# Hybrid diffusion layer on one core: the first stage loads its modulation weights into later h tiles, takes the sample's x first, halves its first block and moves the prompt's norm into its loop

## The chip, the cores and the metric

The kernel runs on one core of one Trainium2 chip. The metric is the device time of one execution in microseconds (us). Matrix products run on TensorE (PE in the profile), elementwise work on VectorE (DVE), ScalarE (ACT) and GpSimd (POOL); transfers are issued from the queue of SyncE (SP) and, for some, from that of ScalarE.

## What is computed

One layer for two groups of tokens that share their weights: 256 prompt tokens and 1024 sample tokens of width 1024. The part of the reference that the change touches is the first norm with its modulation and the first columns of the input projection:

```
def rmsnorm(x, g):
    return x * lax.rsqrt(jnp.mean(x * x, axis=-1, keepdims=True) + EPS) * g

mod_ctx = silu(c_ctx) @ w_ada + b_ada          # prompt's modulation, 6 x 1024
mod_lat = silu(c) @ w_ada + b_ada              # sample's modulation
h = rmsnorm(x, g_norm1) * (1.0 + scale_m) + shift_m
proj = h @ w_in                                # then convolutions, a state space scan,
                                               # an output projection and a gated ConvFFN
```

All arithmetic is float32. A product is made of three: each operand is split into hi (rounded to fp32r) and lo (the rest), and hi·hi, hi·lo and lo·hi are added in PSUM.

## The kernel before

The channels of x lie on partitions: x is eight blocks (k = 0 to 7) of 128 channels, each a tile of 128x1024 for the sample (`xs[k]`) and a quarter of a 128x4x256 tile for the prompt (`xp[k // 4][:, k % 4]`). Everything from line 89 to line 348 is the first stage. It must turn x into h (`hs_hi`, `hs_lo` for the sample, `hp_hi`, `hp_lo` for the prompt), and while it does so it already makes the sample's product with the two first column tiles of w_in (`N_LOOP = 2`, accumulators `pps`).

The front of the stage (lines 92 to 274): four small loads (`sm`, `cst`, `rows`), then the prompt's x (line 246) and the sample's (line 259), all on SP's queue. The prompt's squares and their sums over channels come first (lines 249 to 255). Then each sample tile is squared on ScalarE as it lands (line 261) and added on VectorE; a product with a matrix of ones (line 266) sums over partitions. Lines 271 and 272 make the reciprocal roots `rp` and `rs` with Ln and Exp on ScalarE.

`ada_block(k)` (lines 285 to 304) makes block k's shift and scale: it loads 1 MB of modulation weights into one of two halves of the tile `xq` (line 288, so the load for k waits until block k-2's products have read that half), makes eight small products (line 292), copies the sum (line 295), transposes it (line 298), and reduces and adds it on VectorE (lines 299 to 304, by the helpers at lines 77 and 83) to `mod` and `aff`.

The loop (lines 317 to 348) does for each k: load and split of the two weight tiles (lines 318 to 322), `ada_block(k + 1)`, the sample's x times scale and `rs` on VectorE (line 326, helper at line 80), hi on ScalarE (line 328), lo on VectorE (line 329), twelve products of 512 columns (line 337), and for the prompt a scaling by `rp` at k = 0 and 4 (line 341), hi on ScalarE (342), the value on VectorE (343), and at k = 3 and 7 the lo half on GpSimd (348) and the products for dt (`dtmm`, line 311). Behind the loop come the prompt's dt products and then the projection's column tiles in turn, whose weights are loaded and split by `wload` (lines 155 to 158).

The instructions are put in order for each engine when the kernel is built, by program order and by what is ready in the builder's own estimate; on the chip each engine keeps that order. A tile tag with n buffers hands a buffer on when the last reader of its former tile is done. `after(a, b)` adds an order between two instructions without a semaphore.

Of the kernel before, what the change touches and what calls it, by code (L numbers as in the profile page):

```python
# [6 lines left out]
F32 = mybir.dt.float32  # L7
F32R = mybir.dt.float32r
# [47 lines left out]
def body(nc, tc, A):  # L56
# [35 lines left out]
    dma(sm[:, wff1:], A["sm"][:, wff1:])  # L92
    dma(sm[:, 0:wff0], A["sm"][:, 0:wff0])
# [6 lines left out]
    dma(cst, A["cst"][:, : 128 + 40])  # L100
# [3 lines left out]
    dma(rows, A["rows"])  # L104
# [5 lines left out]
    act(arow, rows[:, 0:1], AF.Exp)  # L110
    ts(arow, arow, -1.0, None, ALU.mult, ALU.bypass)
    sc = T(con, [P, KT, 32], "sc", 1)
    V.memset(sc, 0.0)
    act(sc[:, :, 0:2], smv("cc").rearrange("p (k v) -> p k v", v=2), AF.Silu)
# [127 lines left out]
    xT = A["xT"]  # L242

    xp = [T(cv, [P, 4, TP], "xl", 2) for _ in range(2)]
    for q in range(2):
        dma(xp[q], xT[:, 4 * q:4 * q + 4, 0:TP])
    accp = T(sd, [P, 4, TP], "bc", 4)
    sqp = T(sd, [P, 4, TP], "bc", 4)
    act(accp, xp[0], AF.Square)
    act(sqp, xp[1], AF.Square)  # L250
    tt(accp, accp, sqp, ALU.add)
    tt(accp[:, 0:2], accp[:, 0:2], accp[:, 2:4], ALU.add)
    pr_p = pst()
    for i in range(2):
        nc.tensor.matmul(pr_p[:, 0:TP], ones, accp[:, i], start=i == 0, stop=i == 1)
    xs = [T(sd, [P, TS], "bcs", 4) if k < 4 else T(nrm, [P, TS], "x", 4) for k in range(KT)]
    acc_s = T(sd, [P, TS], "bc", 4)
    for k in range(KT):
        dma(xs[k], xT[:, k, TP:TT])
        q = T(cv, [P, TS], "cv", 4) if k else acc_s  # L260
        sq = act(q, xs[k], AF.Square)
        if k:
            tt(acc_s, acc_s, q, ALU.add)
    pr_s = [psa(), psa()]
    for i in range(2):
        nc.tensor.matmul(pr_s[i], ones, acc_s[:, i * 512:(i + 1) * 512], start=True, stop=True)
    tab = lnexp_table(sq)
    rp = T(cv, [P, TP], "cv", 4)
    rs = T(cv, [P, TS], "cv", 4)
    for r, a, b, src in ((rp, 0, TP, pr_p[:, 0:TP]), (rs, 0, 512, pr_s[0]), (rs, 512, TS, pr_s[1])):  # L270
        after(act(r[:, a:b], src, AF.Ln, scale=1.0 / D, bias=epsc), tab)
        act(r[:, a:b], r[:, a:b], AF.Exp, scale=-0.5)
    wdt = T(sd, [P, 640], "toks", 1)[:, 0:KT * 32].rearrange("p (k r) -> p k r", r=32)
    dma(wdt, A["w_dt"])


    hp_hi = [T(sd, [P, 4, TP], "bc", 4, F32R) for _ in range(2)]
    hp_lo = [T(sd, [P, 4, TP], "bc", 4, F32R) for _ in range(2)]
    hs_hi, hs_lo = [], []
    modv = mod.rearrange("p (b k) v -> p b k v", k=KT)  # L280
    badav = smv("bada").rearrange("p (b k) -> p b k", k=KT)

    xq = T(xy, [P, 4, TS], "xs", 1)

    def ada_block(k):
        wa = [xq[:, 2 * (k % 2) + i].rearrange("p (j c) -> p j c", j=4) for i in range(2)]
        for i in range(2):
            dma(wa[i], A["w_ad1"][k, i])
        pm = psa()
        for j in range(KT):  # L290
            q = 32 * (j % 4)
            nc.tensor.matmul(pm[q:q + 32, 0:2 * P], sc[:, j, :], wa[j // 4][:, j % 4, :],
                             start=j < 4, stop=j >= 4, skip_group_check=True, tile_position=(0, q))
        s = T(cv, [P, 2 * P], "cv", 4)
        act(s, pm[:, 0:2 * P], AF.Copy)
# [9 lines left out]

    def dtmm(pd, ks, h, n):
# [8 lines left out]
    pps = []  # L315
    ada_block(0)
    for k in range(KT):
# [1020 lines left out]
```

## Time and profile before

| what | us |
|---|---|
| median of 3 runs | 1551.56 |
| lowest and highest of the runs | 1550.9, 1554.01 |
| the profiled execution's own time | 1551.87 |
| its span, first to last instruction | 1550.1 |
| mean granted TensorE clock | 0.996 |

The profile is of one execution. Its span is the time from the first to the last instruction; 1.8 us of its time lie outside. A row of a timeline gives the start, the length, the engine, the line, the output and the inputs, how many were merged into the row, and in brackets how long the engine had been idle and what released it.

### The profile page before, as it was taken

Reading aid. Unit: us, or ns where it says so; the run is one execution under the profiler, and the core shown is the slowest. Engines: PE = TensorE matmul, PEld = TensorE weight load, DVE = VectorE, ACT = ScalarE, POOL = GpSimd, SP = SyncE. Lnnn points to the kernel's source line nnn. Section 1 sums busy time; section 2 is a strip of 40 time slices with the busy share of each in tenths; the row PEclk is TensorE's granted clock in tenths of the full one; section 3 lists DMA queues with packets and bytes.
Section 4 is the critical chain, followed back from the end, with each engine's and each line's share of the span. In section 5 each row is a group of like instructions: output and inputs, shape, how many; then the busy total and the mean of one; then the engine's idle time right before and its main releaser. Section 6 shows DMA issues by size and latency. Waiting matters only on the chain. (4 is left out here: it accounts for less than half of the span.)

```text
span 1550.1 us, 22496 instructions
## 1 busy us (share of the span) xinstructions
PE 1506.0 (97%) x8706; PEld 1287.7 (83%) x8706; DVE 1095.9 (71%) x1634; ACT 631.0 (41%) x1002; POOL 515.5 (33%) x289
## 2 busy tenths in 40 slices
PE   4999999999999999999999999999999999999997
PEld 2578887878888888888888888888888888888886
DVE  5765344288887467996666697556679978798696
ACT  6545334165654244433233342333334333433333
POOL 0432321111110003333333333333346554545452
PEclk9999999999999999999999999999999999999999
DMA  8635752444336413221222242122433323342221
GB/s 303 238 109 185 249 204 91 136 143 143 130 123 247 155 66 125 77 69 67 74 68 74 74 159 83 55 67 67 148 121 107 105 90 108 107 155 89 95 79 62
DMA packets 90652, 187.79 MB, mean 121 GB/s; under 512 B 9746, under 2 KB 37298, under 8 KB 90546
## 3 DMA queue, kind: packets, MB, share of 16 engines
q1 hardware_dynamic: 84722, 183.22, 34.8%
q10 hardware_dynamic: 5824, 3.15, 0.7%
q8 instruction: 68, 1.11, 0.3%
q14 instruction: 38, 0.31, 0.1%
HBM read 163.70 MB, written 22.63 MB: 120 GB/s over the span
## 5 line engine op out<-in xcount | busy, mean ns | idle before, releaser
L80 DVE SCALAR_TENSOR_TENSOR cc<-acc,sm,cc 128x504 f32<-128x504 f32 (+5 forms) x836 | 546.1, 665 | 110.8 <-ACT cc L1078 52.6
L77 POOL TENSOR_TENSOR wlo<-raw,whi 128x1024 fp32r<-128x1024 f32 (+2 forms) x91 | 211.5, 2324 | 637.1 <-ACT whi L157 444.2
L157 ACT ACTIVATE whi<-raw 128x1024 fp32r<-128x1024 f32 x97 | 102.6, 1058 | 247.3 <-PE acc L168 191.9
L80 DVE SCALAR_TENSOR_TENSOR x<-dn,mod,x 128x288 f32<-128x288 f32 (+2 forms) x176 | 96.2, 547 | 95.0 <-PE dn L170 94.4
L77 POOL TENSOR_TENSOR dlo<-draw,dhi 128x512 fp32r<-128x512 f32 (+1 forms) x88 | 108.8, 1237 | 89.8 <-ACT dhi L1131 89.7
L77 POOL TENSOR_TENSOR wlx<-raw,whx 128x1024 fp32r<-128x1024 f32 (+2 forms) x36 | 84.6, 2351 | 140.9 <-ACT whx L157 132.2
L166 PE MATMUL acc<-ya,whi 128*128 128x512 f32 (+1 forms) x400 | 119.0, 355 | 0.8 <-ACT cv L894 0.8
L168 PE MATMUL acc<-ya,whi 128*128 128x512 f32 (+1 forms) x400 | 118.9, 355 | 0.0
L170 PE MATMUL acc<-ya,wlo 128*128 128x512 f32 (+1 forms) x400 | 118.9, 354 | 0.0
L170 PE MATMUL acc<-oa,wlo 128*128 128x512 f32 (+1 forms) x400 | 118.8, 354 | 0.0
L168 PE MATMUL acc<-oa,whi 128*128 128x512 f32 (+1 forms) x400 | 118.7, 354 | 0.0
L166 PE MATMUL acc<-oa,whi 128*128 128x512 f32 (+1 forms) x400 | 118.3, 353 | 0.0
L166 PE MATMUL dn<-yb,dhi 128*128 128x288 f32 (+2 forms) x352 | 110.1, 313 | 5.3 <-DVE x L80 4.1
L168 PE MATMUL dn<-yb,dhi 128*128 128x288 f32 (+2 forms) x352 | 109.5, 311 | 0.8 <-POOL yb L77 0.8
L170 PE MATMUL dn<-yb,dlo 128*128 128x288 f32 (+2 forms) x352 | 109.3, 311 | 0.0
L166 PE MATMUL acc<-h,whi 128*128 128x512 f32 x336 | 108.7, 405 | 0.0
L170 PE MATMUL acc<-h,wlo 128*128 128x512 f32 x336 | 105.5, 395 | 0.0
L168 PE MATMUL acc<-h,whi 128*128 128x512 f32 x336 | 105.2, 395 | 0.0
L1131 ACT ACTIVATE dhi<-draw 128x512 fp32r<-128x512 f32 (+1 forms) x88 | 52.9, 602 | 121.8 <-PE dn L168 46.6
L166 PE MATMUL dn<-g,dhi 128*128 128x288 f32 (+2 forms) x304 | 95.1, 313 | 0.0
L168 PE MATMUL dn<-g,dhi 128*128 128x288 f32 (+2 forms) x304 | 94.8, 312 | 0.3 <-POOL g L77 0.3
L170 PE MATMUL dn<-g,dlo 128*128 128x288 f32 (+2 forms) x304 | 94.8, 312 | 0.0
(343 smaller groups left out, 3516.8 us busy)
## 6 DMA issues: line engine op xcount, KB each, us to landing
raw<-in_w_up SPq DMA_DIRECT2D x88, 512.0 KB, 3.2
raw<-in_w_in SPq DMA_DIRECT2D x32, 512.0 KB, 3.4
ws<-in_w_ada SPq DMA_DIRECT2D x64, 256.0 KB, 5.0
draw<-in_w_down SPq DMA_DIRECT2D x64, 256.0 KB, 2.9
xs<-in_w_ad SPq DMA_DIRECT2D x16, 512.0 KB, 4.9
bc<-csds SPq DMA_DIRECT2D x16, 512.0 KB, 4.4
raw<-in_w_out SPq DMA_DIRECT2D x16, 512.0 KB, 3.3
x<-in_xT SPq DMA_DIRECT2D x8, 640.0 KB, 6.0
```

Of the source, the lines that this page charges most:

```text
L77: (eng or V).tensor_tensor(out=out, in0=a, in1=b, op=op)
L80: V.scalar_tensor_tensor(out=out, in0=a, scalar=s, in1=b, op0=op0, op1=op1)
L157: act(hi, raw, AF.Copy)
L166: nc.tensor.matmul(o, wh[:, k, :], rh(k), start=k == 0, stop=False)
L168: nc.tensor.matmul(o, wh[:, k, :], rl(k), start=False, stop=False)
L170: mm = nc.tensor.matmul(o, wl[:, k, :], rh(k), start=False, stop=k == n - 1)
L1131: act(wh, raw, AF.Copy)
```

## The change

In the front, the four small loads go on ScalarE's queue, the table for Ln and Exp is loaded right behind the Silu, and SP's queue begins with the sample's x. `block_loads(k)` loads block k's two weight tiles (all eight blocks' of them lie in `xq[:, 0:2]`, named `raws`) and its modulation weights, which now lie in two tiles of the tag `h` (16 buffers, which later hold `hs_hi` and `hs_lo`). Block 0's loads stand between x tiles 4 and 5; the prompt's x comes behind the sample's; blocks 1 to 3 follow; block k + 4's are issued in iteration k. `ada_block(0)` and block 0's weight split move in among the squares. The last square is not added on VectorE: it is made in two halves and summed by its own products with ones, beside those of the other seven. Block 0's x, hi and lo are made in halves of 512 columns, and its products that need lo come last. The copies of `ada_block` and the weight splits of k >= 1 are ordered behind block 0's hi (`hi0`), and `ada_block(k + 1)`'s products behind block k-1's last product. The prompt's squares follow block 0, its sums and root block 1, and its blocks iterations 2 (0 and 1), 3 (2 and 3) and 4 to 7. The first `wload` is ordered behind the last of `block_loads`.

```diff
-    dma(sm[:, wff1:], A["sm"][:, wff1:])
-    dma(sm[:, 0:wff0], A["sm"][:, 0:wff0])
+    nc.scalar.dma_start(sm[:, wff1:], A["sm"][:, wff1:])
+    nc.scalar.dma_start(sm[:, 0:wff0], A["sm"][:, 0:wff0])
...
-    dma(cst, A["cst"][:, : 128 + 40])
+    nc.scalar.dma_start(cst, A["cst"][:, : 128 + 40])
...
+    loads_end = []
...
         w_dma[0] = dma(raw, src)
+        if loads_end:
+            after(w_dma[0], loads_end.pop())
...
+    tab = lnexp_table(silu_c)
+    after(act(arow, rows[:, 0:1], AF.Exp), tab)
...
+    wa = []
+    xq = T(xy, [P, 4, TS], "xs", 1)
+    raws = xq[:, 0:2].rearrange("p a (b j c) -> p (a b) j c", b=4, j=N_LOOP)
...
+    def block_loads(k):
+        wa.append([T(hsp, [P, TS], "h", 16) for _ in range(2)])
+        dma(raws[:, k], A["w_l"][k])
+        for i in range(2):
+            d = dma(wa[k][i], A["w_ad1"][k, i].rearrange("p j b c -> p (j b c)"))
+        return d
+
+    for k in range(KT):
+        if k == 5:
+            block_loads(0)
+        dma(xs[k], xT[:, k, TP:TT])
     for q in range(2):
         dma(xp[q], xT[:, 4 * q:4 * q + 4, 0:TP])
...
+    for k in range(1, 4):
+        block_loads(k)
     dma(wdt, A["w_dt"])
...
+    halves = [(0, 512), (512, TS)]
+    acc_s = T(sd, [P, TS], "bc", 4)
+    pr_s = [psa(), psa()]
+    for k in range(KT - 1):
+        q = T(cv, [P, TS], "cv", 4) if k else acc_s
+        act(q, xs[k], AF.Square)
+        if k:
+            tt(acc_s, acc_s, q, ALU.add)
+        if k == 5:
+            ada_block(0)
+            w0 = loop_weights(0)
+    q = T(cv, [P, TS], "cv", 4)
+    for a, b in halves:
+        act(q[:, a:b], xs[KT - 1][:, a:b], AF.Square)
+    for src in (acc_s, q):
+        for pp, (a, b) in zip(pr_s, halves):
+            nc.tensor.matmul(pp, ones, src[:, a:b], start=src is acc_s, stop=src is q)
...
+    for k in range(KT):
+        wh, wl = loop_weights(k, hi0) if k else w0
+        x = xs[k]
+        hi, lo = [T(hsp, [P, TS], "h", 16, F32R) for _ in range(2)]
+        cuts = [(0, TS)] if k else halves
+        for a, b in cuts:
+            stt(x[:, a:b], x[:, a:b], aff[:, 0, k, 1:2], rs[:, a:b], ALU.mult, ALU.mult)
+            ci = act(hi[:, a:b], x[:, a:b], AF.Identity, bias=col(0, k, 1))
+        if k == 0:
+            hi0 = ci
+        for a, b in cuts:
+            stt(lo[:, a:b], x[:, a:b], col(0, k, 1), hi[:, a:b].bitcast(F32), ALU.add, ALU.subtract)
...
+        if k < 4:
+            loads_end[:] = [block_loads(k + 4)]
+        if k < KT - 1:
+            ada_block(k + 1, mm, hi0)
+        mms = [(t, n, i) for t in range(N_LOOP) for n in range(3) for i in range(2)]
+        if k == 0:
+            mms.sort(key=lambda v: ((0, 2, 1)[v[1]], v[2]))
+        for t, n, i in mms:
+            wt, ht = ((wh, hi), (wh, lo), (wl, hi))[n]
+            mm = nc.tensor.matmul(pps[t][i], wt[:, t, :], ht[:, i * 512:(i + 1) * 512],
+                                  start=k == 0 and n == 0, stop=k == KT - 1 and n == 2)
+        if k == 0:
+            accp = prompt_squares()
+        if k == 1:
+            pr_p = psa()
+            for i in range(2):
+                nc.tensor.matmul(pr_p[:, 0:TP], ones, accp[:, i], start=i == 0, stop=i == 1)
+            root(rp, 0, TP, pr_p[:, 0:TP], hi0)
+        for kp in {2: (0, 1), 3: (2, 3), 4: (4,), 5: (5,), 6: (6,), 7: (7,)}.get(k, ()):
+            prompt_block(kp)
```

`prompt_squares` and `prompt_block` hold the former lines 249 to 252 and 341 to 348, `root` the former 271 and 272, `loop_weights` the former 320 to 322.

## Rows read from the trace of the kernel before

**Rows 1.** The page's busy times, and the windows view of core 0: stretches of the span with the busy time of PE, PEld, DVE, ACT and POOL (instructions in brackets), then the granted TensorE clock, the DMA engines' share and GB/s.

```profile
span 1550.1 us, 22496 instructions
...
29.24:72.48 43.24, 39.95 (x242) 22.76 (x246) 31.17 (x45) 21.34 (x33) 16.79 (x9) 1.00 0.69 247
...
72.48:78.50 6.02, 6.02 (x75) 5.66 (x75) 5.36 (x8) 4.52 (x8) 3.17 (x3) 1.00 0.69 242
...
4.00:19.00 15.00, 2.07 (x4) 1.17 (x4) 8.24 (x9) 11.17 (x12) 0.00 (x0) 1.00 1.03 392
...
100.00:200.00 100.00, 100.00 (x671) 80.64 (x670) 48.69 (x69) 43.53 (x57) 30.28 (x12) 1.00 0.60 200
```

**Rows 2.** The timeline of SP's queue (issues of transfers).

```profile
0.74 0.39 SPq L92 DMA_DIRECT2D sm<-in_sm  x1
...
2.12 0.41 SPq L104 DMA_DIRECT2D rows<-in_rows  x1
2.58 0.94 SPq L246 DMA_DIRECT2D xl<-in_xT  x2
...
53.03 12.15 SPq L155 DMA_DIRECT2D bcs<-in_w_in  x4
```

**Rows 3.** ScalarE's timeline in the front: table loads, first and last squares (the eight at line 261 run from 9.93 to 20.07), the roots and the first hi.

```profile
2.66 1.28 ACT L114 ACT_TABLE_LOAD   x1 [2.66 <-DMA sm<-in_sm]
...
6.73 1.06 ACT L249 ACTIVATE bc<-xl 128x1024 f32<-128x1024 f32 x1 [1.04 <-DMA xl<-in_xT]
...
19.01 1.06 ACT L261 ACTIVATE cv<-x 128x1024 f32<-128x1024 f32 x1 [0.27 <-DMA x<-in_xT]
20.09 1.28 ACT L225 ACT_TABLE_LOAD   x1
21.38 0.47 ACT L271 ACTIVATE cv<-yp,epsc 128x256 f32<-128x256 f32 x1
21.89 0.42 ACT L272 ACTIVATE cv<-cv 128x256 f32<-128x256 f32 x1
...
23.67 0.69 ACT L271 ACTIVATE cv<-sa,epsc 128x512 f32<-128x512 f32 x1 [1.05 <-PE sa L266]
24.39 0.63 ACT L272 ACTIVATE cv<-cv 128x512 f32<-128x512 f32 x1
...
30.56 1.15 ACT L328 ACTIVATE h<-bcs,mod 128x1024 fp32r<-128x1024 f32 x1 [0.77 <-DVE bcs L80]
```

**Rows 4.** TensorE's timeline in the front, and a later sum with ones of the same kind (line 235: two records of 512 and two of 256 columns; the next product starts at 560.38). A float32 product leaves two records.

```profile
11.29 2.07 PE L255 MATMUL yp<-bc,ones 128*128 128x256 f32 x4 [11.29 <-DVE bc L77]
21.56 3.78 PE L266 MATMUL sa<-bc,ones 128*128 128x512 f32 x4 [8.20 <-DVE bc L77]
25.27 2.45 PE L292 MATMUL sa<-xs,sc 128*32 128x256 f32 x26
...
31.76 1.21 PE L337 MATMUL acc<-h,whi 128*128 128x512 f32 x4 [1.51 <-ACT h L328]
...
559.24 1.49 PE L235 MATMUL dn<-nacc,ones 128*128 128x512 f32 x4
560.38 0.58 PE L166 MATMUL acc<-ob,whx 128*128 128x512 f32 x1
```

**Rows 5.** VectorE's timeline: the prompt's and the sample's adds, the scaling by `rp`, and the loop's blocks 0 and 1.

```profile
9.28 1.23 DVE L77 TENSOR_TENSOR bc<-bc,bc 128x1024 f32<-128x1024 f32 x1 [3.42 <-ACT bc L250]
10.54 0.69 DVE L77 TENSOR_TENSOR bc<-bc 128x512 f32<-128x512 f32 x1
12.30 9.21 DVE L77 TENSOR_TENSOR bc<-bc,cv 128x1024 f32<-128x1024 f32 x7 [1.06 <-ACT cv L261]
22.34 2.89 DVE L77 TENSOR_TENSOR xl<-xl,cv 128x1024 f32<-128x1024 f32 x2 [0.83 <-ACT cv L272]
...
29.24 1.28 DVE L80 SCALAR_TENSOR_TENSOR bcs<-bcs,aff,cv 128x1024 f32<-128x1024 f32 x1
...
31.30 1.28 DVE L80 SCALAR_TENSOR_TENSOR bcs<-bcs,aff,cv 128x1024 f32<-128x1024 f32 x1
```

**Rows 6.** The waits view of 0 to 73 us: who waited for whom, total, times, longest.

```profile
PEld sa L292 <- DMA xs<-in_w_ad: 0.7, 2, 0.4
```

**Rows 7.** Timelines of VectorE and GpSimd around the lo halves of the sample's blocks 2 and 3 and of the prompt's first four blocks.

```profile
39.84 1.28 DVE L80 SCALAR_TENSOR_TENSOR h<-bcs,mod,h 128x1024 fp32r<-128x1024 f32 x1 [0.89 <-ACT h L328]
...
43.72 2.40 POOL L77 TENSOR_TENSOR bc<-xl,bc 128x1024 fp32r<-128x1024 f32 x1 [2.01 <-DVE xl L83]
44.54 2.67 DVE L80 SCALAR_TENSOR_TENSOR h<-bcs,mod,h 128x1024 fp32r<-128x1024 f32 x1 [0.90 <-ACT h L328]
```

**Rows 8.** The windows view from block x to block x in the loop (VectorE's first instruction of blocks 5 and 6).

```profile
54.40:58.78 4.38, 4.34 (x30) 2.37 (x30) 3.38 (x6) 2.47 (x4) 0.74 (x1) 1.00 1.00 390
58.78:65.14 6.36, 6.36 (x42) 4.26 (x44) 4.71 (x6) 2.97 (x4) 2.54 (x1) 1.00 0.32 127
```

**Rows 9.** The end of the loop on TensorE and the weights of the third column tile behind it on ScalarE and GpSimd.

```profile
72.42 1.07 PE L311 MATMUL sa<-xl,toks 128*32 128x256 f32 x16
...
79.97 0.73 PE L166 MATMUL acc<-h,whi 128*128 128x512 f32 x2
...
74.27 1.07 ACT L157 ACTIVATE whi<-bcs 128x1024 fp32r<-128x1024 f32 x1
...
75.42 2.42 POOL L77 TENSOR_TENSOR wlo<-bcs,whi 128x1024 fp32r<-128x1024 f32 x1 [2.85 <-ACT whi L157]
```

More of the change, by code (lines that the diff above doesn't have):

```diff
@@ L245, in body @@
     for q in range(2):
         dma(xp[q], xT[:, 4 * q:4 * q + 4, 0:TP])
[L247 to L272, printed above, removed]
@@ L289, in ada_block @@
+    dma(wdt, A["w_dt"])
+    def ada_block(k, behind=None, copy_behind=None):
         pm = psa()
@@ L291, in ada_block @@
             q = 32 * (j % 4)
-            nc.tensor.matmul(pm[q:q + 32, 0:2 * P], sc[:, j, :], wa[j // 4][:, j % 4, :],
-                             start=j < 4, stop=j >= 4, skip_group_check=True, tile_position=(0, q))
+            mm = nc.tensor.matmul(pm[q:q + 32, 0:2 * P], sc[:, j, :],
+                                  wa[k][j // 4].rearrange("p (j c) -> p j c", j=4)[:, j % 4, :],
+                                  start=j < 4, stop=j >= 4, skip_group_check=True, tile_position=(0, q))
+            if behind is not None:
+                after(mm, behind)
         s = T(cv, [P, 2 * P], "cv", 4)
-        act(s, pm[:, 0:2 * P], AF.Copy)
+        cp = act(s, pm[:, 0:2 * P], AF.Copy)
+        if copy_behind is not None:
+            after(cp, copy_behind)
         tp = pst()
@@ L304, in ada_block, with loop_weights, root @@
         ts(aff[:, 0, k], modv[:, 1, k], 1.0, smv("g1")[:, k:k + 1], ALU.add, ALU.mult)
+    def loop_weights(k, behind=None):
+        wh, wl = [w[:, 0:N_LOOP] for w in wpair()]
+        cast = act(wh, raws[:, k], AF.Copy)
+        if behind is not None:
+            after(cast, behind)
+        tt(wl, raws[:, k], wh.bitcast(F32), ALU.subtract, nc.gpsimd)
+        return wh, wl
+    def root(r, a, b, src, prev):
+        after(act(r[:, a:b], src, AF.Ln, scale=1.0 / D, bias=epsc), prev)
+        return act(r[:, a:b], r[:, a:b], AF.Exp, scale=-0.5)
+    halves = [(0, 512), (512, TS)]
[15 more added lines that the diff above has]
+            nc.tensor.matmul(pp, ones, src[:, a:b], start=src is acc_s, stop=src is q)
+    rp = T(cv, [P, TP], "cv", 4)
+    rs = T(cv, [P, TS], "cv", 4)
+    prev = tab
+    for pp, (a, b) in zip(pr_s, halves):
+        prev = root(rs, a, b, pp, prev)
+    hs_hi, hs_lo, hp_hi, hp_lo = [], [], [], []
     def dtmm(pd, ks, h, n):
@@ L313, in dtmm, with prompt_squares, prompt_block @@
                                  tile_position=(0, q))
[L315 to L338 removed]
+    def prompt_squares():
+        accp = T(sd, [P, 4, TP], "bc", 4)
+        sqp = T(sd, [P, 4, TP], "bc", 4)
+        after(act(accp, xp[0], AF.Square), hi0)
+        act(sqp, xp[1], AF.Square)
+        tt(accp, accp, sqp, ALU.add)
+        tt(accp[:, 0:2], accp[:, 0:2], accp[:, 2:4], ALU.add)
+        return accp
+    def prompt_block(k):
         q, i = k // 4, k % 4
         if i == 0:
+            hp_hi.append(T(sd, [P, 4, TP], "bc", 4, F32R))
             tt(xp[q], xp[q], rp.unsqueeze(1).broadcast_to([P, 4, TP]), ALU.mult)
```

53 lines of the change are left out of this document (15 added, 38 removed).

## The prediction

> **What bounds the kernel now.** I read the page's busy times first: TensorE is busy for nearly the whole span of 1550.1 us. By the windows view it stays so from the end of the loop on: 6.02 of 6.02 us behind the loop and 100.00 of 100.00 later [rows 1]. So behind the first stage a gain or loss of that stage passes through in full, as long as the first projections find their weights. Before it, things differ. The first product of the loop starts at 31.76 [rows 4], and until then TensorE does a few small sums. The change is worth what it does to two times: that of this first product, and the length of the loop behind it, which from block 0's first VectorE instruction to the end takes 43.24 us [rows 1].
>
> What sets 31.76? The timelines of the front, read backwards: hi of block 0 at 30.56 [rows 3], block 0's x at 29.24 [rows 5], which needs `rs` and the modulation of block 0. The second root ends at about 26.7 (Ln and Exp behind the first pair, which starts at 23.67 [rows 3]); the modulation products start only at 25.27, behind the sums with ones in TensorE's queue [rows 4], although their weights had long landed. So block 0's modulation ends last, about 2.5 us behind the roots. The sums start at 21.56, and the last square starts at 19.01 behind ten loads of 0.5 MB, the two of the prompt first. These move the DMA engines at 392 GB/s with share 1.03 [rows 1]: the front is bound by transfers up to 20, then by a chain.
>
> In the loop the waits view shows 0.7 us in which products waited for modulation weights [rows 6]. What paces a block is the chain through TensorE: last products of block k-1, modulation products of k+1, copy, transposes, VectorE's three small instructions, x of k+1. Blocks cost 4.38 us where nothing interferes and 6.36 where GpSimd's subtract stands in the way [rows 8]. TensorE is busy 39.95 of the 43.24 us, VectorE 31.17, ScalarE 21.34 [rows 1].
>
> **The front, step by step.** (1) SP's queue loses four issues: its first x is issued at 0.74 and not at 2.58, 1.84 us earlier [rows 2]. The issues go to ScalarE, four of about 0.41, ahead of its first table load, which until now waits for `sm` until 2.66. Two table loads of 1.28 and two short activations follow, so ScalarE is free for squares at about 6 where the first x is there at about 6.73 - 1.84 = 4.9 [rows 3]. A square takes 1.06 and a tile arrives each 1.3, and block 0's loads make a pause of 2.9 us (1.18 MB at 392 GB/s), so the late start is caught up: 0. Without the pause it would cost about 1 us.
> (2) Ahead of the last x tile stand 8 tiles and block 0's 1152 KB in place of 10 tiles, 128 KB more: 0.3 us. The last x lands at 19.01 - 1.84 + 0.3 = 17.5.
> (3) The last square is made in halves (about 0.6 each, by the 0.63 of a 512-column Exp) and ends at 18.1 and 18.7. The add of the seven ends at about 18.6: the seventh tile lands at 16.2, and a square (1.06) and an add (9.21/7 = 1.3 [rows 5]) follow. One add of 1.3 leaves the chain.
> (4) The sums double: eight records in place of four. In the old front four take 25.27 - 21.56 = 3.71 us, 0.93 each; later in the kernel two of 512 and two of 256 columns take 560.38 - 559.24 = 1.14, or 0.38 for 512 [rows 4]. The granted-clock column says 1.00 for both stretches, but the records show the lower level (1.2 GHz) in the front, after 8.2 us in which TensorE did nothing, and the upper (2.4 GHz) later, in dense work. Block 0's modulation now runs at about 13 to 16, then TensorE is idle again until 18.6. I take the low level for the first four records (to 22.3) and leave the level open for the next two: the first half's sum is done at 23.1 to 24.2 and its Ln, 0.25 later as now, starts at 23.3 to 24.4.
> The page "TensorE: Matmul & The Clock Gate" of the Trainium skill (Part 1, The HAM clock gate) says that the array's default is the low clock and that sustained work releases it; it speaks against doubling sums right behind a pause. The old front agrees with it: 0.93 against 0.38 us for a record.
> (5) Ln, Exp (0.69 + 0.63 with gaps: 1.35), half of x (0.65, half of 1.28) and half of hi (0.6, half of 1.15) give block 0's first product at 26.0 to 27.2, middle 26.6. Against 31.76 that is **5.1 us earlier**, by 4.6 to 5.8. Block 0's modulation is covered by the squares: its weights land at about 13, and copy, transposes and the small VectorE instructions end before 18. If the builder had put it behind the sums again, 3.97 us (25.27 to 29.24) less 2.5 would be lost.
>
> **The loop, step by step.** (6) Block 1's modulation loses its lead: its copy is ordered behind `hi0`, so its x starts at about 29.5 (31.30 now [rows 5]), only 1.8 us earlier. From there the chain is DVE 1.28, ACT 1.15: block 1's first product at about 32.2, some 4 us earlier. Whether this 1.1 us is lost depends on TensorE, which still has block 0's products and block 2's modulation to do until about 31: 0 to 1.1, I take 0.3.
> (7) The prompt's sums move into TensorE's chain behind block 1: 2.07 us for four records in the old front [rows 4], half of it at the rate of a warmed-up engine: 1.0, bounds 0 (TensorE idles 3.3 in the loop) to 2.07. I take 1.0, since they stand right in front of block 3's modulation.
> (8) VectorE gets 1.23 + 0.69 + 2.89 = 4.8 us more in the loop [rows 5]. It idles 12.1 of 43.24 us; so 0 to 4.8 is exposed. TensorE is what paces most blocks, so I take a quarter, 1.2.
> (9) ScalarE gets two squares (1.06 each) and the prompt's root (0.47 + 0.42 [rows 3]). It idles half of the loop: 0, or up to 1.06 where a square stands before block 2's copy.
> (10) The modulation weights have tiles of their own, so their loads no longer wait for products two blocks back: -0.7, the whole wait [rows 6]. Blocks 1 to 5 need no wait for a tile and land from 23 on, one each 2.9 us. On SP's queue block 6's load waits for block 1's modulation products and block 7's for block 3's (at about 37). Behind these stand the first `wload` transfers, which can't start earlier anyway: they need the x tiles that dt reads (53.03 now for the second [rows 2]). Nothing that is needed before 60 waits there: 0, and if the cover is gone, the third column tile shows it first, whose lo half ends at 75.42 + 2.42 = 77.8 for products at 79.97 [rows 9], 2.1 us of slack.
> (11) The halves of block 0 cost four more instruction overheads, under 0.3, in an order in which hi products run meanwhile: 0. Six column tiles behind the loop are unchanged.
>
> Sum: -5.1 + 0.3 + 1.0 + 1.2 - 0.7 = **-3.3**. The profiled execution took 1551.87, the median is 1551.56, 0.3 less; I set it against the median: **1548.2**. The bounds of the terms (-5.8 to -4.6, 0 to 1.1, 0 to 2.07, 0 to 4.8, 0 to 1.06, -0.7 to 0) give -6.5 to +4.4; not all end at one side.
>
> **Rivals.**
> *The loop gets shorter too.* With all weights in place the blocks could run at 4.38 us [rows 8] more often: the intervals now average (65.14 - 29.24)/7 = 5.1. If the prompt's work falls into VectorE's idle time and two of the seven intervals lose a us each, the sum is -5.8 + 0.5 - 0.7 - 2 = -8: about 1543.5 (1540.5 to 1545.5). For it: 12.1 us idle on VectorE. Against: the waits for weights, which the change removes, are only 0.7.
> *All is given back.* The prompt's VectorE work lies on the chain in full: -5.1 + 0.3 + 1.0 + 4.8 - 0.7 = +0.3: 1551.9 (1550 to 1554). For it: x, lo and the small instructions of a block wait in the same queue, and order is fixed at build time. Against: TensorE, not VectorE, ended most of the waits.
> *Slower: VectorE becomes the bound through GpSimd.* Block 3's lo half took 2.67 and not 1.28 because GpSimd's 2.40 us subtract was running: it ended about 1.1 us after it [rows 7]. GpSimd is busy 16.79 us in the loop. The four moved two-input instructions meet it now, which none did at 9 to 25. If each is held for 1.4 as that one was, and all of it is exposed, +0.3 + 4 x 1.4 = +5.9: about 1557 (1554.7 to 1559). It decides from the point where VectorE's 31.2 + 4.8 plus the holds fill the shorter loop of some 42 us, four holds of 1.4.
> The page "GPSIMD Engine Reference" of the Trainium skill (Specifications) says that GpSimd shares its SBUF interfaces with VectorE and contends with its instructions of two SBUF inputs, which speaks for this rival; the 2.67 us agrees.
> *It doesn't do what it says:* if the order puts block 0's modulation behind the sums, front and loop give -3.6 + 1.8, within the second rival's range.
>
> **How the numbers follow.** Forecast (1545.5 to 1550.5) 0.5, shorter loop 0.2, given back 0.2, slower 0.1. A measurement of this kernel can't tell less than about 0.2%, 3.1 us, from no change: below 1548.5 is faster, above 1554.7 slower. Of the forecast's half about 0.35 lies below 1548.5, with the shorter loop 0.55. Slower: 0.11. Same: 0.34. The range of 8 in 10 leaves out the slower rival and the tail of the shorter loop: 1542.5 to 1553.0.
>
> **What would show it.** After: first x issue at 0.74 on SP; last square at about 17.5; block 0's first product at 26 to 27; block 1's x near 29.5; loop end (line 311's prompt products, 72.42 now [rows 9]) at 68 to 70; VectorE's idle time in the loop cut by some 4 us. The forecast is wrong if block 0's first product is later than 28, if VectorE instructions of the prompt stand directly before an x or lo half with TensorE idle, or if the first projections wait for weights.

## The result, and the profile after

The changed kernel takes 1557.57 us (median of 7 runs, 1556.22 to 1561.43) against 1551.56 (7 runs, 1550.9 to 1555.46): ratio 1.004, interval 1.0027 to 1.0052. It is slower by some 6 us, where 3.4 less were forecast. One execution of run a13 below took 3017.16 us and is left out of its row.

The front did what it should. From the timelines of SP, ScalarE and TensorE in the changed kernel, one after the other (columns as in the rows ahead of the prediction):

```profile
0.74 2.11 SPq L269 DMA_DIRECT2D bcs<-in_xT  x4
```

```profile
5.15 1.28 ACT L112 ACT_TABLE_LOAD   x1 [5.15 <-DMA sm<-in_sm]
...
18.09 1.15 ACT L325 ACTIVATE cv<-x 128x512 f32<-128x512 f32 x2 [0.25 <-DVE bc L77]
24.05 0.69 ACT L308 ACTIVATE cv<-sa,epsc 128x512 f32<-128x512 f32 x1 [4.82 <-PE sa L328]
...
26.01 0.63 ACT L309 ACTIVATE cv<-cv 128x512 f32<-128x512 f32 x1
26.55 0.71 ACT L376 ACTIVATE h<-bcs,mod 128x512 fp32r<-128x512 f32 x1
```

```profile
19.79 3.37 PE L328 MATMUL sa<-bc,ones 128*128 128x512 f32 x4 [2.21 <-DVE bc L77]
22.99 1.88 PE L328 MATMUL sa<-cv,ones 128*128 128x512 f32 x4
24.80 1.07 PE L280 MATMUL sa<-h,sc 128*32 128x256 f32 x16
27.30 0.74 PE L392 MATMUL acc<-h,whi 128*128 128x512 f32 x2 [1.43 <-ACT h L376]
```

SP's first x is issued at 0.74 [rows 2]; the first half of the last square starts at 18.09 (the whole one stood at 19.01 [rows 3]); eight records of sums, four slow and four fast, end at about 24.8; block 0's first product is at 27.30, 4.46 earlier than 31.76 [rows 4].

The loop takes it back. Three marks of TensorE's timeline are used from here on: block 0's first product (A), block 2's first product (B), and the first of the prompt's dt products, where the loop ends (C). Before: 31.76, 40.05, 72.42. After: 27.30, 39.42, 75.74. By block 2, 3.83 of the 4.46 are gone, and from there to the end another 3.95. The windows view, A to B and B to C, before and after (columns: us, then each engine's busy time with its instructions, the granted clock as a share of full speed, DMA share, GB/s):

```profile
31.76:40.05 8.29, 8.29 (x50) 5.21 (x50) 6.19 (x10) 4.28 (x7) 0.74 (x1) 1.00 0.72 264
40.05:72.42 32.37, 30.61 (x182) 17.21 (x179) 22.52 (x31) 15.26 (x25) 15.99 (x8) 1.00 0.67 239
```

```profile
27.30:39.42 12.12, 11.29 (x65) 7.09 (x65) 10.31 (x15) 7.61 (x13) 4.32 (x4) 0.86 0.94 357
39.42:75.74 36.32, 33.90 (x182) 17.56 (x178) 24.62 (x36) 16.82 (x28) 13.68 (x7) 1.00 0.46 159
30.00:32.00 2.00, 2.00 (x6) 1.58 (x5) 2.00 (x2) 1.98 (x4) 1.27 (x2) 0.50 1.04 402
```

From A to B VectorE is now busy 10.31 of 12.12 us (6.19 of 8.29 before), with hardly a gap from 26.67 to 37.31 by its timeline, and from 30 to 32 TensorE's granted clock is 0.50, its lower level (1.2 GHz), after two waits of 1.43 and 0.47 around block 0's first products. VectorE's timeline of block 1:

```profile
29.66 1.28 DVE L80 SCALAR_TENSOR_TENSOR bcs<-bcs,aff,cv 128x1024 f32<-128x1024 f32 x1
30.86 1.77 DVE L77 TENSOR_TENSOR bc<-bc,bc 128x1024 f32<-128x1024 f32 x1
32.66 1.10 DVE L77 TENSOR_TENSOR bc<-bc 128x512 f32<-128x512 f32 x1
33.69 1.76 DVE L80 SCALAR_TENSOR_TENSOR h<-bcs,mod,h 128x1024 fp32r<-128x1024 f32 x1
35.37 0.16 DVE L292 TENSOR_REDUCE mod<-yp 128x4 f32<-128x16 f32 x1
35.57 0.16 DVE L77 TENSOR_TENSOR mod<-mod,sm 128x4 f32<-128x4 f32 x1
35.77 0.23 DVE L83 TENSOR_SCALAR aff<-mod,sm 128x2 f32<-128x2 f32 x1
36.03 1.28 DVE L80 SCALAR_TENSOR_TENSOR bcs<-bcs,aff,cv 128x1024 f32<-128x1024 f32 x1
```

The reader is to see the queue: the prompt's two adds stand between x and lo of block 1, and block 2's small instructions and x behind lo. All three large ones are longer than usual (1.77, 1.10, 1.76 for 1.23, 0.69 and 1.28 [rows 5]). From B on, the difference that meets the eye is in the dt products of TensorE's timeline. Blocks 4 to 7 before (line 311), then all of them after (line 343):

```profile
56.57 1.02 PE L311 MATMUL sa<-x,toks 128*32 128x512 f32 x2
...
64.96 3.42 PE L311 MATMUL sa<-x,toks 128*32 128x512 f32 x14
```

```profile
44.82 1.94 PE L343 MATMUL sa<-bcs,toks 128*32 128x512 f32 x14
...
49.45 1.90 PE L343 MATMUL sa<-x,toks 128*32 128x512 f32 x4 [1.56 <-DVE x L80]
...
58.62 1.88 PE L343 MATMUL sa<-x,toks 128*32 128x512 f32 x4
...
64.52 1.88 PE L343 MATMUL sa<-x,toks 128*32 128x512 f32 x4
...
69.99 1.91 PE L343 MATMUL sa<-x,toks 128*32 128x512 f32 x4
...
75.74 1.07 PE L343 MATMUL sa<-xl,toks 128*32 128x256 f32 x16
```

Fourteen records of four blocks take 1.94 together; the four records of one block alone take as long. Blocks 4 to 7 now stand alone, each behind its x: 7.6 us in place of 4.4 before.

Behind the loop the distance of matching products from before's is 3.2 to 3.6 us until 339, 6.2 from 346 and 8.2 from 970: in the profiled run (1560.22) TensorE waits longer there and has more of its time at the lower clock (0.84 from 340 to 350, 0.83 from 960 to 980; before 1.00 and 0.91). The mean granted clock differs from run to run (0.993 to 0.998 in the 7 runs). So the loop's end, +3.3 of the +6, is what is explained here; the other 2.7 are not.

### The profile page after: what moved, and what is told of

It reads as the page before. It is cut to its first block, busy times and chain, and to the rows that moved or that the text cites. A ratio compares the mean times of both kernels' runs of the same rounds, so it can differ in the third digit from the quotient of the medians.

```text
span 1558.4 us, 22494 instructions
## 1 busy us (share of the span) xinstructions
PE 1513.3 (97%) x8710; PEld 1290.9 (83%) x8710; DVE 1094.7 (70%) x1635; ACT 628.4 (40%) x1003; POOL 515.2 (33%) x289
## 5 line engine op out<-in xcount | busy, mean ns | idle before, releaser
L77 POOL TENSOR_TENSOR wlo<-raw,whi 128x1024 fp32r<-128x1024 f32 (+1 forms) x85 | 204.5, 2406 | 599.3 <-ACT whi L159 425.7
L77 POOL TENSOR_TENSOR wlx<-raw,whx 128x1024 fp32r<-128x1024 f32 (+1 forms) x34 | 82.2, 2418 | 140.8 <-ACT whx L159 138.3
```

What stands on the lines that cost most here:

```text
L77: (eng or V).tensor_tensor(out=out, in0=a, in1=b, op=op)
```

## The experiments

The table holds the runs with the three marks (us); A to C is the loop. The edits and expectations follow. A ratio stands against runs of the kernel before on the same chip, whose median lay between 1551.56 and 1553.55, so the ratios can be compared, the medians less well. In e4 and e8 the prompt's dt products are mixed with the sample's, so they have no C; there the first projection's start (73.52 before) is used.

| run | A | B | C | A to B | B to C | median | ratio (interval) |
|---|---|---|---|---|---|---|---|
| before | 31.76 | 40.05 | 72.42 | 8.29 | 32.37 | 1551.56 | |
| after | 27.30 | 39.42 | 75.74 | 12.12 | 36.32 | 1557.57 | 1.004 (1.0027 to 1.0052) |
| e1 | 27.47 | 41.18 | 77.89 | 13.71 | 36.71 | 1557.83 | 1.0033 (1.0021 to 1.0045) |
| e2 | 30.36 | 40.49 | 74.55 | 10.13 | 34.06 | 1554.0 | 1.0005 (0.9996 to 1.0014) |
| e3 | 28.36 | 39.84 | 75.43 | 11.48 | 35.59 | 1557.53 | 1.0026 (1.0013 to 1.0039) |
| e5 | 29.68 | 39.81 | 72.77 | 10.13 | 32.96 | 1553.8 | 1.001 (1.0 to 1.0019) |
| e6 | 31.51 | 40.96 | 77.61 | 9.45 | 36.65 | 1557.14 | 1.0028 (1.0017 to 1.004) |
| e7 | 28.17 | 38.28 | 73.99 | 10.11 | 35.71 | 1554.48 | 1.0013 (1.0003 to 1.0024) |
| e9 | 28.11 | 38.23 | 71.20 | 10.12 | 32.97 | 1553.83 | 1.0005 (0.9994 to 1.0017) |
| e10 | 29.70 | 39.82 | 74.80 | 10.12 | 34.98 | 1556.45 | 1.0018 (1.0004 to 1.0032) |
| e11 | 28.49 | 38.89 | 71.34 | 10.40 | 32.45 | 1552.35 | 1.0001 (0.9987 to 1.0016) |
| e12 | 30.77 | 40.11 | 72.32 | 9.34 | 32.21 | 1554.46 | 1.0002 (0.9989 to 1.0014) |
| a13 | 28.80 | 40.30 | 74.70 | 11.50 | 34.40 | 1554.08 | 1.0015 (1.0003 to 1.0027) |
| a14 | 28.25 | 40.35 | 77.03 | 12.10 | 36.68 | 1558.88 | 1.0042 (1.0026 to 1.0057) |
| a15 | 29.82 | 39.24 | 73.24 | 9.42 | 34.00 | 1554.42 | 1.0015 (1.0001 to 1.0028) |
| b16 | 30.21 | 40.28 | 71.49 | 10.07 | 31.21 | 1551.17 | 0.9987 (0.9978 to 0.9996) |

Two things limit all of them. The builder orders each engine anew, so an edit can move other instructions too; where it did, it is said. And the marks of a run come from one execution. In after, e1 and a14 every engine does the same instructions in the same order up to B, and yet A is 27.30, 27.47 and 28.25 and B 39.42, 41.18 and 40.35. Before, e4 and e12 have the same order on TensorE, VectorE and ScalarE up to B, and A is 31.76, 31.86 and 30.77. In a14 it was the sums that ran slower (TensorE's timeline; 3.37 and 1.88 in after):

```profile
19.47 3.78 PE L328 MATMUL sa<-bc,ones 128*128 128x512 f32 x4 [2.10 <-DVE bc L77]
23.04 3.14 PE L328 MATMUL sa<-cv,ones 128*128 128x512 f32 x4
```

So a difference of about 1 us between two runs' marks says little by itself, and one of 1.8 can come from where the clock falls.

**e1 and e4: the dt products.** e1 is the changed kernel with blocks 4 to 7's dt products put together; e4 is the kernel before with each of them alone.

```diff
# e1
-            dtmm(pd_s, range(k - 3, k + 1), lambda k: xs[k], TS)
+            dtmm(pd_s, range(k - 3, k + 1), lambda k: xs[k], TS, prev_mm)   # behind block k-1's last product
```

```diff
# e4
+        if k == 3:
+            dtmm(pd_s, range(4), lambda k: xs[k], TS)
+        if k > 3:
+            dtmm(pd_s, [k], lambda k: xs[k], TS, mm)   # behind block k's last product
...
-            dtmm(pd_s, range(k - 3, k + 1), lambda k: xs[k], TS)
```

> The changed kernel, with the dt products of the sample's blocks 4 to 7 ordered behind the last product of block 6, so that they stand nearly together instead of one pair in each of four blocks. Theory D (scattered dt products lengthen the loop): a pair alone takes 1.9 us in the changed kernel's trace and fourteen records of four blocks together take the same 1.94, so TensorE loses some 4 to 5.5 us of work in the loop; the median falls from 1557.6 to 1552 to 1553.6 and the loop's end from 75.7 to 70.5 to 72. Rival P (the prompt's norm work in the loop on VectorE and TensorE is the cause): less than 1.5 us changes, 1556 to 1558. Rival C (TensorE's low clock in block 0 is the cause): also less than 1.5 us.

> The kernel before, with the dt products of the sample's blocks 4 to 7 each made right behind their own block. Theory D: four pairs of 1.9 us stand in the place of one pair and seven products together, so 2 to 4 us slower than before: 1553.5 to 1555.5. Rivals P and C: no change, 1551.0 to 1552.5.

e4 went the way of theory D, by more than its 2 to 4 us: 1557.99, ratio 1.0034 (1.0021 to 1.0047), the first projection 3.2 later than before's. e1 missed: A is the same, the dt products are together (x6 and x10, 1.90 and 1.92), and yet C is 2.15 later. TensorE waited 1.88 and 2.63 for lo of blocks 1 and 3, and behind both waits ran at the lower clock (0.50 from 37 to 40 and from 54 to 57). Putting the dt products together did not help while TensorE waited for VectorE; 1.76 of the 2.15 stand at B already, up to which the order is that of the changed kernel, so they are not the edit's.

**e2 and e5: the prompt's norm in front.** Its x is loaded first, squares, adds, sums and root precede the loop, and each iteration takes one prompt block; e2 also has e1's edit, e5 leaves dt to the builder, which puts 14 records into one run of 3.44 (3.42 before).

```diff
+    for q in range(2):
+        dma(xp[q], xT[:, 4 * q:4 * q + 4, 0:TP])     # ahead of the sample's x
...
-        if k == 0:
-            accp = prompt_squares()
...
+        prompt_block(k)
```

> As the first kernel, and the prompt's x is loaded first again, with its squares, sums and root in the front and its blocks one in each iteration, as before the change. Theory D: the front's first product comes about 2.6 us later (27.3 to about 30), the loop sheds 1.0 us of sums and part of 4.8 us on VectorE, so the result is within 1.5 us of the first kernel. Rival P: the loop gets shorter by the full 5.8, so it is 2 to 4 us faster than the first kernel.

> The changed kernel with only the prompt's norm moved back in front of the loop: its x tiles loaded first, its squares, adds, sums and root made ahead of the last sum, one prompt block in each iteration; the dt products are left to the builder (in its order block 4's first record stands alone, seven others together). The chain theory (the prompt's adds and scalings are what pushed the loop out on VectorE): first product about 30.4 as with the dt products pinned (30.36), loop 44 us or less against 48.4 in the changed kernel and 40.7 before, loop end near 74, time 1552.5 to 1554.5. The dt theory (lone dt records cost 1.9 us each and are what slowed the loop): since this build has few lone ones, it too expects a gain, but of the same size as in the run where only the dt products were put together, so a loop end not under 75.7 and 1556 or more. If both are false the loop end stays near 77.5 (front 3 later) and the time near 1559.

The chain theory holds. In e5 the front gives 2.38 back and the loop is 5.35 shorter (43.09 against 48.44): 1.99 of it from A to B, 3.36 behind. The ratio falls from 1.004 to 1.001, and the intervals do not meet. Pinning the dt products (e2) makes B to C 1.1 longer than in e5. The rest of the change (e5 against before) then gains 2.08 in A and loses 2.43 in the loop, and is worth nothing.

**e10: half of that move.** e5 with the prompt's scalings and blocks where the change has them.

```diff
-        prompt_block(k)
+        for kp in {2: (0, 1), 3: (2, 3), 4: (4,), 5: (5,), 6: (6,), 7: (7,)}.get(k, ()):
+            prompt_block(kp)                       # scalings ordered behind lo of blocks 2 and 3
```

> The version with only the prompt's norm moved back, but with that move halved: squares, adds, sums and root of the prompt in front of the loop, while its two scalings (behind lo of block 2 and of block 3) and its blocks stay where the change put them. Theory that the two adds on VectorE in front of lo of block 1, the sums behind them and the fall of the clock there are the larger part of the 5.3 us by which the prompt's norm lengthens the loop (48.4 against 43.1): the loop comes to about 44, its end to 73.5 to 74.5. Rival, the scalings, the doubled blocks and the dt order that follows from them are the larger part: a loop of 46 or more, its end at 75.7 or later, and the time at 1556 or more.

C came at 74.80, between the two bands; the loop is 45.10. So squares, adds, sums and root inside the loop cost 3.34 (48.44 less 45.10), the scalings, doubled blocks and the dt order that follows from them 2.01 (45.10 less 43.09). The first is the larger part in these traces, by 1.3, which is hardly more than their scatter. The time, 1556.45, lies in the rival's band, but the kernel before took 1553.33 on that chip.

**e3 and a13: the clock.** Three products that no result uses fill TensorE's wait before block 0, in e1 and in the changed kernel.

```diff
+        if k == 0:
+            for _ in range(3):
+                f = nc.tensor.matmul(pps[1][1][:, 0:256], ones, q[:, 512:768], start=True, stop=True)
+                after(f, ada_mm[0])
```

> As the first kernel, and three float32 products of 256 columns, whose result is overwritten and that belong to no output, stand between block 1's modulation products and block 0's first product, where TensorE stood idle for 1.4 us before its clock fell. Theory C (the clock's fall at about 29 us costs 1.7 us in block 0): the granted clock stays at 1.00 from 25 to 35 and the loop's end comes 1 to 2 us earlier than in the first kernel. Rival: the clock falls all the same, or the filler only delays block 0: 0 to 0.7 us later.

> The changed kernel with three products of 256 columns more, which no result uses, between block 1's modulation products and block 0's first product. Theory that the clock's fall at 29.3 to 32.7 comes from TensorE's thin stretch in front of block 0 and costs 1.7 us: no stretch at the lower clock in the loop, block 0's first product up to 1 us later (28.3), the loop end up to 1.7 earlier than 75.74, at 74 to 75.2. Rival, the fall comes later in the loop or the time is waited for VectorE instead: loop end within 0.4 of 75.74 or later.

Neither has a stretch at the lower clock in the loop, and C fell by 2.46 and 1.04. That the products did it is not shown: a14 below has no such stretch either, and no filler. And the clock is not what the changed kernel lost. In a13 B is later (40.30 for 39.42), and the gain lies behind B, where the builder had put the dt products together again:

```profile
58.85 1.02 PE L346 MATMUL sa<-x,toks 128*32 128x512 f32 x2
...
67.20 3.46 PE L346 MATMUL sa<-x,toks 128*32 128x512 f32 x14
...
74.70 1.07 PE L346 MATMUL sa<-xl,toks 128*32 128x256 f32 x16
```

Blocks 4 to 7's records take 1.02 and 3.46 there, 4.5 in place of 7.6, and B to C falls from 36.32 to 34.40: about 1.9 us, which I put down to the lone dt products. The order of other instructions behind B moved too, so in the changed kernel this price is argued; in the kernel before e4 shows it.

**a14, e11 and e12: GpSimd's long subtract.** The prompt's lo in four pieces each, in the changed kernel, in e9 (below) and in the kernel before.

```diff
-            tt(hp_lo[q], xp[q], hp_hi[q].bitcast(F32), ALU.subtract, nc.gpsimd)
...
+        tt(hp_lo[q][:, i], xp[q][:, i], hp_hi[q][:, i].bitcast(F32), ALU.subtract, nc.gpsimd)
```

> The changed kernel with GpSimd's two subtracts for the prompt's lo (128 x 1024, 2.42 each) cut into one of 128 x 256 for each block. Theory of holds: the small instruction at 45.66 that took 2.41 for 0.23 falls under 1, block 4's x starts up to 1.6 earlier than 48.11, the loop ends 1 to 1.6 earlier, 74.1 to 74.7. Rival: the pieces hold other instructions, or TensorE has other work to do meanwhile (the dt products stand there): loop end within 0.4 of 75.74.

> The version with the prompt's norm first and the last square added, with GpSimd's two subtracts of 128 x 1024 for the prompt's lo (2.40 each) cut into one of 128 x 256 for each block. In the version with the prompt's norm first VectorE's lo of block 3 took 3.21 where 1.28 is usual, while the first of these subtracts ran from 44.10 to 46.50, and TensorE then waited 1.69 for it. Theory that a VectorE instruction with two inputs is held until GpSimd's running instruction ends: with short ones no lo takes over 2.1, the wait falls under 0.7 and the loop ends about 1 to 1.5 earlier than without this edit. Rival, the pieces meet more of VectorE's instructions and hold each a little: the loop's end within 0.4 of the version without it, or later. If theory and the earlier front add up, loop end near 70.3 and time near 1551, no slower than the kernel before.

> The kernel before, with GpSimd's two subtracts of 128 x 1024 for the prompt's lo cut into one of 128 x 256 for each block and nothing else. Its lo of block 3 took 2.67 for 1.28 while the first subtract ran, and TensorE's interval there is the longest, 6.70. By the theory of holds the interval falls by about 1.2 and the loop ends at about 71.2 against 72.42; time 1550.5 to 1551.5. Rival: the pieces hold other instructions, loop end 72 to 73, no difference.

VectorE's lo of block 3 in e9 and in e11, which differ by this edit alone:

```profile
42.78 3.19 DVE L80 SCALAR_TENSOR_TENSOR h<-bcs,mod,h 128x1024 fp32r<-128x1024 f32 x1 [1.09 <-ACT h L385]
```

```profile
43.70 1.52 DVE L80 SCALAR_TENSOR_TENSOR h<-bcs,mod,h 128x1024 fp32r<-128x1024 f32 x1 [1.09 <-ACT h L384]
```

This hold is real and goes (3.19 to 1.52; in a14 the small instruction of 2.41 took 0.67), and TensorE's wait of 1.69 with it, but C does not come earlier: 71.34 for 71.20 in e11, 72.32 for 72.42 in e12, 77.03 for 75.74 in a14, where A is 0.95 later. The holds moved instead. In e11 and e12 GpSimd is done sooner and starts the next weight tile's subtract sooner (65.78 in e11, 67.96 in e9), and that one holds block 7's lo for longer, 3.21 us in e11 and 2.55 in e9, 3.22 in e12 and 2.56 before (VectorE's timeline of e11, then GpSimd's):

```profile
66.02 3.21 DVE L80 SCALAR_TENSOR_TENSOR h<-x,mod,h 128x1024 fp32r<-128x1024 f32 x1 [1.01 <-ACT h L384]
```

```profile
65.78 2.36 POOL L77 TENSOR_TENSOR wlo<-bcs,whi 128x1024 fp32r<-128x1024 f32 x1
```

TensorE waits 1.50 for that lo in e11 and 0.84 in e9. In a14 the pieces hold others: block 3's x took 1.76, and two more small instructions 0.74 and 0.70 for 0.40 and 0.16. So the rival holds in e11 and e12, in a14 neither does, and none of the three shows what a loop without holds would gain. a14 holds a second answer, unplanned: this run had no lower clock in the loop, and A to B took 12.10, as in the changed kernel with it (12.12), because TensorE then waited for lo of block 1 instead (VectorE's timeline of a14, then a row of TensorE's):

```profile
31.80 1.77 DVE L77 TENSOR_TENSOR bc<-bc,bc 128x1024 f32<-128x1024 f32 x1
33.60 1.11 DVE L77 TENSOR_TENSOR bc<-bc 128x512 f32<-128x512 f32 x1
34.64 1.74 DVE L80 SCALAR_TENSOR_TENSOR h<-bcs,mod,h 128x1024 fp32r<-128x1024 f32 x1
```

```profile
36.43 0.73 PE L391 MATMUL acc<-h,whi 128*128 128x512 f32 x2 [1.88 <-DVE h L80]
```

So the fall of the clock from 29.3 on cost nothing by itself: it lay under VectorE's queue. In e1, with the same order, the fall came behind that wait, at 36, where nothing covered it, and A to B took 13.71.

**a15, e6 and b16: the order pins.** Without the pins the builder puts block 1's modulation with its transposes and block 2's products ahead of block 0's first product.

```diff
-            ada_block(k + 1, mm, hi0)
+            ada_block(k + 1)
...
-        wh, wl = loop_weights(k, hi0) if k else w0
+        wh, wl = loop_weights(k) if k else w0
```

> The changed kernel without its order pins on the modulation products, their copy and the loop's weight casts: in the builder's order block 1's products, copy and transposes and block 2's products then stand ahead of block 0's first product, and the dt products of blocks 0 to 3 are less scattered. Theory that the lost lead of the modulation (my step 6, sized 0.3) is one of the larger terms: first interval 6.41 falls to about 4.5, no lower clock in block 0, loop end 73 to 74.5. Rival: block 0's products come later by block 2's products (1.07), and the adds of the prompt on VectorE set the second interval anyway: loop end within 0.5 of 75.74 or later.

> The kernel with dt products pinned and the prompt's norm first, with one more difference: the change's order pins on the modulation products, their copy and the loop's weight casts are gone, and the builder puts the modulation products of blocks 1 and 2 ahead of block 0's first products, as the kernel before had block 1's. Theory that a block's modulation in the loop's chain is what keeps that loop 3.5 us longer than before's (44.2 against 40.7): the intervals of the first two blocks fall from 5.55 and 4.58 to about 4.4 and 4.0, loop end about 73 against 74.55, time about 1552.5. Rival, TensorE is what paces the loop: its work is the same, the time moves from one wait to another, loop end 74.5 within 0.5, time 1554.

> The version with the prompt's norm first, the last square added and GpSimd's subtract by block, with the order pins on the modulation products, their copy and the weight casts gone too. Theory that the pins are what is left of the first two blocks' length: from block 0's first product to block 2's first product 8.3 to 9.2 us against 10.1 to 10.4 with pins; block 2's modulation products stand ahead of block 0's first product, which comes about 0.5 to 1 later than 28.5; loop end about 70.5, time 1551 to 1553. Rival, the two blocks stay at 10 or more because VectorE's and ScalarE's chain of x, hi and the small instructions sets them: loop end 71.5 or later, time 1552.5 or more. In either case it is not over 0.2% faster than the kernel before.

In the changed kernel (a15) A is 2.52 later and A to B 2.70 shorter, for work has moved in front of A: at B nothing is gained (39.24 for 39.42). The gain at C, 2.50, lies behind B, where the dt products are together again (34.00 for 36.32); the ratio is 1.0015 (1.0001 to 1.0028). Block 1's lo and the prompt's adds, from VectorE's timeline:

```profile
29.60 1.29 DVE L80 SCALAR_TENSOR_TENSOR bcs<-bcs,aff,cv 128x1024 f32<-128x1024 f32 x1
30.80 1.41 DVE L80 SCALAR_TENSOR_TENSOR h<-bcs,mod,h 128x512 fp32r<-128x512 f32 x2
32.13 1.22 DVE L77 TENSOR_TENSOR bc<-bc,bc 128x1024 f32<-128x1024 f32 x1
...
33.38 0.69 DVE L77 TENSOR_TENSOR bc<-bc 128x512 f32<-128x512 f32 x1
...
34.86 1.28 DVE L80 SCALAR_TENSOR_TENSOR h<-bcs,mod,h 128x1024 fp32r<-128x1024 f32 x1
36.06 1.28 DVE L80 SCALAR_TENSOR_TENSOR bcs<-bcs,aff,cv 128x1024 f32<-128x1024 f32 x1
```

The adds are no longer held (1.22 and 0.69), lo of block 1 takes 1.28, and block 2's x follows at 36.06, though block 0 began 2.5 later. With the prompt's norm in front nothing is gained without the pins. e6 is e2 without them: A to B is 9.45 for 10.13, but behind a wait of 1.86 the clock fell, and C is 3.06 later, in neither band. b16 is e11 without them: A to B stays at 10.07, as the rival has it, and C is 71.49 for 71.34. b16 is the one version whose interval lies below 1: 1551.17 against 1553.55, ratio 0.9987 (0.9978 to 0.9996), one of sixteen tried, so this is weak evidence. Its front is 1.55 earlier than before's and even that is gone by B (40.28 for 40.05); it gains behind B, 31.21 for 32.37.

**e7 and e9: the doubled sums.** The last square is added by VectorE again, in e2 and in e5.

```diff
+        tt(acc_s[:, a:b], acc_s[:, a:b], q[:, a:b], ALU.add)
...
-    for src in (acc_s, q):
```

> The kernel with dt products pinned and the prompt's norm first, with the last square again added by VectorE, so that four records of sums stay in place of eight. Theory that doubling the sums costs more than the add that it saves: eight records took 2.08 + 1.75 + 1.88 us from 22.17 to 27.9; four at the lower level take about 3.8 behind an add that ends about 1.3 later than the last half square, so block 0's first product would come at about 30.4 - 1.9 + 0.7 = 29.2 and the time about 1553. Rival, the add of 1.3 (in two halves) costs what the records save: first product within 0.4 of 30.36, time 1554.

> The version with only the prompt's norm moved back in front of the loop (dt products left to the builder), with the last square added by VectorE again and four records of sums in place of eight. In the version with pinned dt products this edit brought block 0's first product from 29.68 to 28.17 or 1.5 earlier, but the loop lost it again to a fall of the granted clock near 46 to 50. Theory that the front's gain passes through when the clock stays up: first product 28.2, loop end 71.3 against 72.77, time about 1552.5. Rival, an earlier front makes the loop wait: loop end within 0.4 of 72.8 and the time as with doubled sums, 1553.8.

A falls by 2.19 and 1.57 (1.2 and 1.5 were expected): eight records cost more than the add that they save. In e9 the gain reaches C in full (71.20 for 72.77); in e7 a wait of 1.70 for lo of block 3 was followed by the lower clock, which took most of it. The ratios (1.0005 and 1.001) cannot tell e9 from e5.

**e8: dt last.** In e6, all dt products behind block 6's last product.

```diff
-        if k % 4 == 3:
-            dtmm(pd_s, range(k - 3, k + 1), lambda k: xs[k], TS, prev_mm)
+            dtmm(pd_s, range(KT), lambda k: xs[k], TS, prev_mm)     # at k == 7
```

> The kernel with early modulation products, with all dt products of the loop in one piece: those of blocks 0 to 3 too are pinned behind block 6's last product. Theory that each lone dt record costs TensorE time of its own (1.9 us for what takes 0.14 in company): in the kernel with early modulation three records of blocks 0 and 1 stand between other products, so this one ends the loop up to 2 us earlier. Rival: those lone records stand in front of products that wait for VectorE anyway, so nothing is gained, within 0.5 at the loop's end. Against the kernel before this is the version with the best chance to be no slower: 1551 to 1553.

It took 1560.21, ratio 1.0048 (1.0032 to 1.0065). Its first projection stands at 74.26, 4.45 ahead of e6's, more than expected, and 0.7 behind before's, but the products near 173 are 6.1 late: the move was paid for behind the loop, by waits of TensorE for weights' lo (0.6) and dt's chain (1.9) and by one more stretch at the lower clock. What of it weighs how much was not separated.

## Why the prediction was wrong

*Front, steps 1 to 5: right in kind, 0.6 short.* Forecast 5.1 earlier, measured 4.46. The last square began at 18.09 (17.5 forecast). Step 3 was 1.1 short: the add of the seven ended at 19.74 and not at 18.6, behind block 0's small instructions in VectorE's queue (VectorE's timeline):

```profile
17.98 0.17 DVE L292 TENSOR_REDUCE mod<-yp 128x4 f32<-128x16 f32 x1
...
18.52 1.22 DVE L77 TENSOR_TENSOR bc<-bc,cv 128x1024 f32<-128x1024 f32 x1
```

The sums made most of that good, 3.37 and 1.88 for the eight, so that the first Ln began at 24.05 (23.3 to 24.4 forecast). The last 0.4 was lost on ScalarE, whose queue has the second root, until 26.64, ahead of the first hi at 26.55; its x was there at 26.19. The better part of the sums is luck, for in a14 the same eight took 3.78 and 3.14. A record took 0.84 us behind the pause and 0.47 next, though the granted-clock column reads 1.00 for both. The page "TensorE: Matmul & The Clock Gate" of the Trainium skill (Part 1, The HAM clock gate), by which the lower clock is the default and activity ends it, agrees with these lengths. Doubling the sums was a loss: without it A is 1.6 to 2.2 earlier (e9, e7).

*Step 8 failed first.* It counted a quarter (1.2) of VectorE's 4.8 us as exposed, since "TensorE is what paces most blocks". From A to B VectorE does (its queue above, and a14), and with step 7 (1.0) and step 9 (0) the prompt's norm cost 5.35 in place of 2.2 (e5). The rival "all is given back" had this mechanism.

*Left out altogether: the dt products.* The moved blocks and x tiles changed where the builder puts them. The price is shown in the kernel before (e4, 3.2); in the changed kernel it is about 1.9 (a13), part of the 5.35.

*Step 6 mis-sized.* Block 1's x came at 29.66 as forecast (29.5). Its first product came at 33.71, but at 32.34 in e1, where the clock had not yet fallen (32.2 forecast). Yet blocks 0 and 1 take 10.1 even with the prompt's norm in front, 1.8 more than before. The 0.3 was 1.8; what makes it was not separated: without the pins they take 9.4 in e6 and e8, with work moved in front of A, and 10.07 in b16. In the changed kernel taking the pins away moves C by 2.50, behind B (a15). Such terms don't add up: each edit also changes the place of the dt products.

*Steps 10 and 11.* The 0.7 of step 10 was not gained. The waits view of the changed kernel, from 24 to 76, still has one such wait (0.7 in two before [rows 6]), at 32.62:

```profile
PEld sa L280 <- DMA h<-in_w_ad: 0.7, 1, 0.7
```

It stands before block 2's modulation, while TensorE still had block 0's products to do, so it is not seen as a loss either.

The sum, at C: forecast -3.3, measured +3.3. Of the 6.6 between them 0.6 is the front, 3.1 the prompt's norm (5.35 less 2.2), 2.8 the rest of the loop (2.43 measured, -0.4 forecast), each to about 1 us, the scatter of the marks.

*The slower rival gave the right time (1557), by luck: its holds were a quarter of what it took.* GpSimd did hold VectorE's adds and lo of block 1, 1.4 us in all (0.54, 0.41 and 0.48), not four times 1.4, and the scalings not at all (1.22 and 1.21; before, where the rival has no hold, they took 2.89 [rows 5] beside a subtract of GpSimd at 22.70). The 1.4 us lie in the queue that paces A to B, so they may be part of what was lost there; no run takes them away alone. Over the whole loop the lengths beyond the usual add up to some 4.5 us on VectorE before and 5.8 after, an estimate from the two timelines: holds were there before, too. The page "GPSIMD Engine Reference" of the Trainium skill (Specifications) agrees with the holds, 1.77 against 1.22.

Open: why the lower clock comes after some waits (1.43 and 0.47 here; 1.70 in e7) and not after others as long (1.70 in e2, 1.88 in a14), and how much of the 2.7 us beyond the loop's end is more of it in later stages.

## What to carry to other kernels

A front that ends earlier is worth what the next stage can take: look up which engine's queue paces that stage's first blocks, not its mean over the stage, before work is moved into it. Cost every instruction whose place depends on the moved ones, even where the diff does not touch it: here the dt products. Where a builder makes the order, an order pin is a change of its own: taking the pins away moved C by -2.5, +3.1 and +0.1 in three versions. And let two builds with the same order up to a mark show how far that mark scatters, before a difference of 1 us is explained.

## What was not expected of the hardware

- The four records of one block's dt products (32 columns of weights, 512 columns each) take 1.90 us; fourteen records of four blocks, each on its own quarter of the array's columns, take 1.94 together (after, blocks 0 to 3), but 3.42 in another run of fourteen (before, blocks 4 to 7). What makes this difference is open.
- GpSimd also held a VectorE instruction of 128x2 with a scalar from SBUF (TENSOR_SCALAR at 45.66, 2.41 for 0.23) until its own subtract (45.63, 2.42) ended. Cut into pieces (a14), the subtract held several instructions for less each.
- `sm`, loaded from ScalarE's queue beside the x tiles, released its reader at 5.15; on SP's queue ahead of them it had been 2.66 [rows 3]. The squares started at 9.14, where 6 had been forecast, and caught up: the last began at 18.09, or 17.41 in e1.
